# ConvFFN input part: five orders of the products of high and low parts, in turn by group of blocks

## Chip, cores and metric

The kernel runs on one core of one Trainium2 chip. The metric is the device time of one execution in microseconds. The kernel before takes 892.87 us, the median of 3 runs (892.58 to 893.33).

## The reference, cut to what matters

The program computes one layer of a hybrid encoder block on 512 frames of 1024 channels: two recurrent branches, a merge, cross-attention, and a gated ConvFFN, with a norm ahead of each and one at the end. The change lies in the input half of the ConvFFN:

```
def conv_ffn(h, w_in, conv_w, conv_b, w_out):
    u = h @ w_in                                  # (512 x 1024) @ (1024 x 5632)
    gate = causal_dwconv(u[..., :D_FF], conv_w, conv_b)
    return (jax.nn.gelu(gate) * u[..., D_FF:]) @ w_out
```

`D_FF` is 2816: a gate half and a value half of 22 blocks of 128 columns each. What is changed is in which order the matmuls of `h @ w_in` are issued.

## The kernel before

**Precision.** Each float32 operand is split into a high part (rounded to the matmul's input format) and a low part (the remainder). A product is made of three matmuls: high by high, high by low and low by high. `mm3` (line 165) issues the three in this order, with the weights first in each pair: lines 166 (weights high, moving operand high), 167 (weights high, moving operand low) and 168 (weights low, moving operand high). Each matmul comes with a load of its own weights.

**Seven products.** The input part multiplies in a Strassen-like scheme: the activations and weights are cut into two by two parts and seven products of sums of these are made instead of eight. Each product has a name by its weights: `A11`, `s1`, `s2`, `s4`, `s3`, `A12`, `A22`; the table `RHS` (line 1206) gives the activation operand of each (`hop`, tiles `hq` and `hr` in the profile, with high and low part of 4 tiles of 128x256 each).

**Groups.** The loop at line 1258 goes through the 22 blocks in 11 groups of `NQ = 2`. In a group, each product is made for block 0 and then for block 1. One product of one block is 4 steps in depth by 3 matmuls, 12 matmuls of 128x128 weights by 256 columns. So a group has 7 x 2 x 12 = 168 matmuls. The accumulators are in PSUM, for each block: `X` (`fx_ps`, 256 columns) and `YZ` (`fyz_ps`, 512 columns). `X` collects in turn A11, s2, s3 and A22, the second half of `YZ` s1 and s4, the first half A12. There are four of each, so that two groups are in flight. Between products the running state is copied out: ScalarE copies `X` after A11 (line 1266) and after s2 (line 1274) to `sn`, and the half of `YZ` after s1 (line 1269) to `p5`; VectorE adds `X` after s3 to `p5` (line 1279). Each next product onto the same tile must wait for that copy: s2 for 1266, s4 for 1269, s3 for 1274, A22 for 1279.

**Behind a group** VectorE and ScalarE make the convolution over time, the gelu (line 1293, ScalarE) and the product of gate and value (lines 1286 to 1297) while TensorE works on the next group.

**Weights.** `stream_quarters` (line 124) makes one load for each product of a group, that is, for both blocks: a DMA to `wfi_r` (four buffers), a cast on ScalarE to the high part `wfi_h` (line 132), a subtraction on VectorE for the low part `wfi_l` (line 133), three buffers each. A buffer is free for the load after next-but-one when TensorE has read it for the last time.

**Background sums.** The sums of weight parts for the coming products are made by accumulating DMAs on POOL. `sum_behind` (line 173) ties the next of these to a matmul, which paces them.

**Order.** A scheduler of the language orders the instructions of each engine by their dependencies, their place in the program and its own estimate of times; loads and their casts have high priority. The queues of the engines are worked off in that order.

Of the kernel before, what the change touches and what calls it, by code (L numbers as in the profile page):

```python
# [12 lines left out]
ALU = mybir.AluOpType  # L13
# [4 lines left out]
P = 128  # L18
T = 512
# [39 lines left out]
def hybrid_block_kernel(ctx: ExitStack, tc: tile.TileContext, xT_d, mT_d, pv_d, cst_d, win_d, wk_d, wv_d,  # L59
                        lup_d, gup_d, rga_d, rgx_d, wba_d, wbb_d, wmix_d, wq_d, wo_d, wfi_d, wfo_d, out_d):  # L60
    nc = tc.nc
    V, S, PE = nc.vector, nc.scalar, nc.tensor
# [26 lines left out]
    def par(name, i, n=1):  # L89
        o = PV[name][0]  # L90
        return pv[:, o + i:o + i + n]
# [32 lines left out]
    def stream_quarters(srcs, name):  # L124

        for g, src in enumerate(srcs):
            with tc.high_priority():
                raw = wp.tile([P, 2, T], F32, tag="wr", name=f"{name}_r{g}", bufs=4)
                wdma.append(nc.sync.dma_start(raw, src))
                hi = wp.tile([P, 2, T], F32R, tag="wh", name=f"{name}_h{g}")  # L130
                lo = wp.tile([P, 2, T], F32R, tag="wl", name=f"{name}_l{g}")
                S.copy(hi, raw)  # L132
                V.tensor_tensor(lo, raw, hi.bitcast(F32), ALU.subtract)  # L133
            for i in range(2):
                yield hi[:, i], lo[:, i]

    class Units:
# [10 lines left out]
        def next(self):  # L148
            if self.left == 0:
                self.fill()  # L150
            i = self.i
            self.i += 1
            self.left -= 1
            return self.hi[:, i * P:(i + 1) * P], self.lo[:, i * P:(i + 1) * P]
# [10 lines left out]
    def mm3(ps, lh, ll, rh, rl, start, stop, **kw):  # L165
        first = PE.matmul(ps, lh, rh, start=start, stop=False, **kw)  # L166
        PE.matmul(ps, lh, rl, start=False, stop=False, **kw)  # L167
        PE.matmul(ps, ll, rh, start=False, stop=stop, **kw)  # L168
        return first
# [3 lines left out]
    def sum_behind(ins, n=1):  # L173

        for put in islice(sums, n):
            tc.add_manual_dep(tc.keep_in_program_order(put()).ins, ins.ins.name, mybir.DependencyInfo(
                mybir.DependencyClass.Sync, mybir.DependencyReason.DATA), reason="pace of the sums")
# [89 lines left out]
    def rstd_bc(out, ssq, n, pool=None, scratch=None, load=True, split=None, **kw):  # L267

        ps = rw_ps("rs_ps", pool, **kw)
        if split is None:  # L270
            PE.matmul(ps[:, :n], ones, ssq, start=True, stop=True)
        else:
            sum_exact(ps[:, :n], onesr, ssq, *split)
        rsqrt(out, ps[:, :n], 1.0 / D, eps[:, 0:1], load)
        if scratch is not None:
            newton(out, ps[:, :n], scratch, 1.0 / D, 1e-6)
# [6 lines left out]
    with tc.tile_pool(name="p0", bufs=1, reuse_waits="tile") as p0:  # L283
# [103 lines left out]
        for hf in range(2):  # L387
            pss = [(mm_ps if hf else rw_ps)(f"v_ps{hf}_{i}") for i in range(2)]
            for k2 in range(4):
                wh, wl = next(st)  # L390
                for kk in range(2):
                    kb = 2 * k2 + kk
                    rh, rl = wh[:, kk * T:(kk + 1) * T], wl[:, kk * T:(kk + 1) * T]
                    for i in range(2):
                        sl = slice(i * P, (i + 1) * P)
# [72 lines left out]
    NQ = 2  # L468
# [269 lines left out]
    with tc.tile_pool(name="pz", bufs=1, reuse_waits="tile") as pz:  # L738
# [9 lines left out]
        for s in range(30, -1, -1):  # L748
            n = 31 - s
# [25 lines left out]
    for i0 in (0, 16):  # L775
# [3 lines left out]
        for i in range(16):  # L779
            for e in range(2):  # L780
                r, k = rows[0][e], rows[1][e]
                PE.matmul(psh[e][k, i * 32:(i + 1) * 32], BZ[r, i0 + i, 32:64], ZA[r, i0 + i, :],
                          start=True, stop=True)
        for e, copy in enumerate((S.copy, V.tensor_copy)):
            k = rows[1][e]
            copy(Hs[e][k], psh[e][k].rearrange("p (i t) -> p i t", t=32))
        for i in range(16):
            for e in range(2):
                r, k = rows[0][e], rows[1][e]
                PE.matmul(pso[e][r, i * 32:(i + 1) * 32], Hs[e][k, i, :], BZ[k, i0 + i, 32:64],  # L790
                          start=True, stop=True)
        for e, copy in enumerate((S.copy, V.tensor_copy)):
            r = rows[0][e]
# [355 lines left out]
    H = T // 2  # L1149
# [19 lines left out]
    for m in order:  # L1169
# [5 lines left out]
        i = m % 4  # L1175
# [32 lines left out]
    def source(m, n):  # L1208
        if n[0] == "A":
            return quarter(m, int(n[1]), int(n[2]), NQ)  # L1210
        return dS[m // NQ][:, :, SLOT[n], :].rearrange("n p f -> p n f")

    wq = stream_quarters([source(m, n) for m in range(0, FB, NQ) for n in RHS], "wfi")

    def product(n, out, start, nsum=0):
        wh, wl = next(wq)
        b = hop[RHS[n]]
        for i in range(4):
            sl = slice(i * P, (i + 1) * P)
            ins = mm3(out, wh[:, sl], wl[:, sl], b[:, 0, i, :], b[:, 1, i, :], start and i == 0, i == 3,  # L1220
                      skip_group_check=not start)
            if i < nsum:
                sum_behind(ins)

    graw = pc.tile([P, FB, T], F32, name="graw", bufs=1)
    gsets = [[pc.tile([P, n, 2, H], F32R, name=f"go0_{n}", bufs=1) for n in (8, 3)], [None, None], [None, None]]
# [7 lines left out]
    def split_g(i, src, k):  # L1236
        dst, n = part(i, k)
        S.copy(dst[:, :, 0, :], src(slice(k, k + n)))
        V.tensor_tensor(dst[:, :, 1, :], src(slice(k, k + n)), dst[:, :, 0, :].bitcast(F32), ALU.subtract)

    def g1(ks, c):
        return graw[:, ks, (c - 1) * H:c * H]
# [7 lines left out]
    def b1_g(k):  # L1250
        ks = slice(k, min(k + 4, HB))
        diff_g(g1(ks, 1), g1(ks, 1), g1(ks, 2))

    def b3_g(k):
        ks = slice(k, min(k + 4, HB))
        diff_g(g1(ks, 2), g2(ks, 2), g1(ks, 2))

    for m0 in range(0, FB, NQ):
        ms = range(m0, m0 + NQ)
        YZ = {m: pf.tile([P, T], F32, tag="yz", name=f"fyz_ps{m}", bufs=4) for m in ms}  # L1260
        X = {m: pf.tile([P, T], F32, tag="x", name=f"fx_ps{m}", bufs=4)[:, 0:H] for m in ms}
        sn = {m: pc.tile([P, T], F32, tag="sn", name=f"sn{m}", bufs=3) for m in ms}
        p5 = {m: pc.tile([P, H], F32, tag="p5", name=f"p5_{m}", bufs=3) for m in ms}
        for m in ms:
            product("A11", X[m], True, nsum=m - m0)
            S.copy(sn[m][:, 0:H], X[m])
        for m in ms:
            product("s1", YZ[m][:, H:T], True)
            S.copy(p5[m], YZ[m][:, H:T])
        if m0 == 0:  # L1270
            rstd_bc(rf, ssf, T, pf, split=(pc, "ac", "rf"), tag="yz", bufs=4)
        for m in ms:
            product("s2", X[m], False, nsum=m - m0)
            S.copy(sn[m][:, H:T], X[m])
        for m in ms:
            product("s4", YZ[m][:, H:T], False, nsum=m - m0)
        for m in ms:
            product("s3", X[m], False)
            V.tensor_tensor(p5[m], X[m], p5[m], ALU.add)
        for m in ms:  # L1280
            product("A12", YZ[m][:, 0:H], True, nsum=m - m0)
        for m in ms:
            product("A22", X[m], False, nsum=(m - m0) * (m0 // NQ % 2))
        for m in ms:
            s = pc.tile([P, T], F32, tag="s", name=f"fs{m}")
            V.tensor_tensor(s, YZ[m], sn[m], ALU.add)
            V.tensor_tensor(s, s, rf, ALU.mult)
            ac = pc.tile([P, T], F32, tag="ac", name=f"fa{m}")
            S.activation(ac, s, AF.Identity, scale=par("fcw", 44 + m), bias=par("fcb", m))
            for k in range(1, 3):  # L1290
                V.scalar_tensor_tensor(ac[:, k:], s[:, 0:T - k], par("fcw", 22 * (2 - k) + m), ac[:, k:],
                                       ALU.mult, ALU.add)
            gelu = S.activation(ac, ac, AF.Gelu_apprx_tanh)
            V.tensor_tensor(ac, ac, rf, ALU.mult)
            out = graw[:, m]
            V.scalar_tensor_tensor(out[:, 0:H], X[m], -1.0, ac[:, 0:H], ALU.mult, ALU.mult)
            V.scalar_tensor_tensor(out[:, H:T], p5[m], -1.0, ac[:, H:T], ALU.mult, ALU.mult)
            k = m % HB
            if k % 4 == 3 or k == HB - 1:
                k -= k % 4  # L1300
                if m < HB:
                    split_g(0, lambda ks: g1(ks, 1), k)
                    b1_g(k)
                else:
                    b3_g(k)
# [61 lines left out]
    X = [pf.tile([P, T], F32, tag="x", name=f"ox_ps{m}", bufs=4)[:, 0:H] for m in range(MQ)]  # L1367
    YZ = [pf.tile([P, T], F32, tag="yz", name=f"oyz_ps{m}", bufs=4) for m in range(MQ)]
    cols = (slice(0, H), slice(H, T))
    sn1, sn5 = ([pc.tile([P, T], F32, tag="sn", name=f"{n}_{i}", bufs=3) for i in range(2)] for n in ("o1", "o5"))  # L1370
    p1, p5 = ([t[:, c] for t in ts for c in cols] for ts in (sn1, sn5))
# [158 lines left out]
```

## Time and profile before

| what | value |
|---|---|
| median of 3 runs | 892.87 us |
| profiled execution, span | 892.8 us |
| TensorE busy | 877.4 us, 98% |
| VectorE busy | 685.2 us, 77% |
| ScalarE busy | 513.6 us, 58% |
| input part of the ConvFFN (first matmul of group 0 to first matmul of the output part) | 553.83 to 772.65 us |
| in it: matmuls of the products | 1848 |

All times are of one core. The profiled execution has no time of its own beside its span; the span agrees with the median to 0.1 us. The busy time of TensorE counts pipelined matmuls, so the distance between the starts of two matmuls is the cost of one and not its recorded duration. In lists in order of time the columns are the start in us, the duration in us, the engine, the line, the operation, output and inputs, shapes and count, and in brackets how long the engine was idle before it and what ended that.

### The profile page before, as it was taken

The numbers are of one execution on the slowest core, as the hardware profiler recorded it, in microseconds if no ns is written. First come the engines' busy times: TensorE is split into PE (matmuls) and PEld (weight loads), VectorE is DVE, ScalarE is ACT, GpSimd is POOL, SyncE is SP. The second block draws the span as 40 slices with busy tenths as digits, with TensorE's granted clock in tenths as the row PEclk, the third lists the DMA queues.
The fourth block names the chain that finished last, engine by engine and source line by source line (L and its number), as shares of the span: only waits on it lengthen the run. The fifth ranks groups of instructions, "written<-read, shape, count | busy, mean of one in ns | idle before, by whom it ended". The sixth has DMA issues, their size and how long they took to land.

```text
span 892.8 us, 15934 instructions
## 1 busy us (share of the span) xinstructions
PE 877.4 (98%) x6197; PEld 767.9 (86%) x6197; DVE 685.2 (77%) x1104; ACT 513.6 (58%) x783; POOL 132.5 (15%) x163
## 2 busy tenths in 40 slices
PE   8999999999999999999999999999999999999996
PEld 7878878888877677888888778999999999999996
DVE  6796598777967677675575578889888889999674
ACT  6575676634347676233554466766655656757563
POOL 0101222021102021001122111111111111211100
PEclk9999999999999999999999999999999999999999
DMA  7878899678997279758888958999999999998963
GB/s 268 307 253 215 206 228 233 187 203 233 262 227 156 72 203 249 220 166 229 218 234 183 197 137 185 260 275 271 265 255 294 263 297 275 244 276 220 261 202 94
DMA packets 97242, 201.37 MB, mean 226 GB/s; under 512 B 19536, under 2 KB 30928, under 8 KB 97104
## 3 DMA queue, kind: packets, MB, share of 16 engines
q1 hardware_dynamic: 62240, 118.57, 40.4%
q0 software_dynamic: 25504, 67.38, 36.9%
q10 hardware_dynamic: 9424, 14.42, 4.7%
q8 instruction: 48, 0.79, 0.4%
q14 instruction: 26, 0.21, 0.1%
HBM read 188.54 MB, written 78.12 MB: 299 GB/s over the span
## 4 chain that ended last, share of the span: by engine, by line
PE 91%; DVE 4%; DMA 2%; ACT 1%; issue 1%; DVEq 0%; ACTq 0%; SPq 0%
PE in_ps L167 7%; PE in_ps L166 7%; PE in_ps L168 7%; PE fx_ps L167 5%; PE fx_ps L166 5%; PE fx_ps L168 5%; PE fyz_ps L167 4%; PE fyz_ps L166 4%; PE fyz_ps L168 3%; PE ox_ps L166 2%; PE oyz_ps L166 2%; PE ox_ps L168 2%; PE oyz_ps L168 2%; PE oyz_ps L167 2%; PE ox_ps L167 2%; PE co_ps L167 2%
## 5 line engine op out<-in xcount | busy, mean ns | idle before, releaser
L132 ACT CAST wfi_h<-wfi_r 128x1024 fp32r<-128x1024 f32 x77 | 81.1, 1053 | 71.5 <-PE fx_ps L167 19.7
L168 PE MATMUL in_ps<-hT,win_l 128*128 128x512 f32 x304 | 121.3, 399 | 0.0
L167 PE MATMUL in_ps<-hT,win_h 128*128 128x512 f32 x304 | 121.0, 398 | 0.2 <-DVE hT L384 0.2
L166 PE MATMUL in_ps<-hT,win_h 128*128 128x512 f32 x304 | 120.6, 398 | 0.3 <-DVE pr L586 0.3
L133 DVE TENSOR_TENSOR wfi_l<-wfi_r,wfi_h 128x1024 fp32r<-128x1024 f32 x77 | 94.1, 1222 | 22.7 <-ACT wfi_h L132 22.4
L482 POOL DMA_DIRECT2D dS<-in_wfi x66 | 66.7, 1028 | 293.1 <-PE in_ps L166 102.3
L167 PEld LDWEIGHTS in_ps<-hT,win_h 128*128 128x128 f32 x304 | 57.1, 188 | 14.2 <-issue 0.7
L166 PEld LDWEIGHTS in_ps<-hT,win_h 128*128 128x128 f32 x304 | 57.1, 188 | 13.2 <-DVE pr L586 0.7
L168 PEld LDWEIGHTS in_ps<-hT,win_l 128*128 128x128 f32 x304 | 57.1, 188 | 13.1 <-issue 0.7
L518 POOL DMA_DIRECT2D dOs<-in_wfo x54 | 39.8, 784 | 181.5 <-PE fyz_ps L166 54.0
L118 DVE TENSOR_TENSOR win_l<-win_r,win_h 128x1024 fp32r<-128x1024 f32 x38 | 46.3, 1221 | 24.2 <-ACT win_h L117 20.7
L117 ACT CAST win_h<-win_r 128x1024 fp32r<-128x1024 f32 x38 | 39.9, 1050 | 41.1 <-PE in_ps L167 32.4
L1341 DVE TENSOR_TENSOR wfo_l<-wfo_r,wfo_h 128x1024 fp32r<-128x1024 f32 (+1 forms) x39 | 47.2, 1209 | 15.2 <-ACT wfo_h L1340 15.2
L1340 ACT CAST wfo_h<-wfo_r 128x1024 fp32r<-128x1024 f32 (+1 forms) x39 | 40.5, 1039 | 31.3 <-DMA wfo_r<-dOs 11.6
L168 PE MATMUL ox_ps<-go,wfo_l 128*128 128x256 f32 x176 | 49.1, 279 | 0.8 <-DVE wfo_l L1341 0.8
L166 PE MATMUL ox_ps<-go,wfo_h 128*128 128x256 f32 x176 | 49.2, 279 | 0.4 <-ACT wfo_h L1340 0.3
L166 PE MATMUL fx_ps<-hq,wfi_h 128*128 128x256 f32 x176 | 49.4, 280 | 0.0
L166 PE MATMUL fyz_ps<-hq,wfi_h 128*128 128x256 f32 x176 | 49.2, 280 | 0.0
L167 PE MATMUL fx_ps<-hq,wfi_h 128*128 128x256 f32 x176 | 49.2, 280 | 0.0
L167 PE MATMUL fyz_ps<-hq,wfi_h 128*128 128x256 f32 x176 | 49.2, 280 | 0.0
L167 PE MATMUL fx_ps<-hr,wfi_h 128*128 128x256 f32 x176 | 49.2, 280 | 0.0
L166 PE MATMUL fx_ps<-hr,wfi_h 128*128 128x256 f32 x176 | 49.2, 279 | 0.0
(432 smaller groups left out, 2704.9 us busy)
## 6 DMA issues: line engine op xcount, KB each, us to landing
dS<-in_wfi POOLq DMA_DIRECT2D x66, 512.0 KB, 7.8
wfi_r<-dS SPq DMA_DIRECT2D x44, 512.0 KB, 6.8
win_r<-in_win SPq DMA_DIRECT2D x38, 512.0 KB, 5.3
wfi_r<-in_wfi SPq DMA_DIRECT2D x33, 512.0 KB, 5.8
dS<-dS POOLq DMA_DIRECT2D x22, 512.0 KB, 5.7
dOs<-in_wfo POOLq DMA_DIRECT2D x12, 512.0 KB, 7.9
wk_r<-in_wk SPq DMA_DIRECT2D x8, 512.0 KB, 5.1
wv_r<-in_wv SPq DMA_DIRECT2D x8, 512.0 KB, 4.0
```

Of the source, the lines that this page charges most:

```text
L117: casts.append(S.copy(hi[:, o:o + n], raw[:, o:o + n]))
L118: V.tensor_tensor(lo[:, o:o + n], raw[:, o:o + n], hi[:, o:o + n].bitcast(F32), ALU.subtract)
L132: S.copy(hi, raw)
L133: V.tensor_tensor(lo, raw, hi.bitcast(F32), ALU.subtract)
L166: first = PE.matmul(ps, lh, rh, start=start, stop=False, **kw)
L167: PE.matmul(ps, lh, rl, start=False, stop=False, **kw)
L168: PE.matmul(ps, ll, rh, start=False, stop=stop, **kw)
L482: return lambda: nc.gpsimd.dma_start(s(out), src, **kw)
L518: yield lambda k=k, w=w, src=src: nc.gpsimd.dma_start(dO[n, m][:, k * P:(k + w) * P], src, **kw)
L1340: S.copy(hi[:, :n], raw[:, :n])
L1341: V.tensor_tensor(lo[:, :n], raw[:, :n], hi[:, :n].bitcast(F32), ALU.subtract)
```

## The change

The function `product` (one block, one product, through `mm3`) is replaced by `products`, which takes both blocks. The weights of both are fetched ahead of the first matmul (they come from one load). A table gives five orders of the 12 matmuls; a pair `(w, r)` names weights and moving operand, 0 for high and 1 for low, and `i` is the step in depth. The group's number modulo 5 picks the order, the *kind*:

- kind 0 (groups 0, 5, 10): for each `i` high-high, high-low, low-high, as before
- kind 1 (groups 1, 6): for each `i` high-high, low-high, high-low
- kind 2 (groups 2, 7): for each `i` high-high, high-low; then low-high for all `i`
- kind 3 (groups 3, 8): high-high for all `i`, high-low for all `i`, low-high for all `i`
- kind 4 (groups 4, 9): the order of kind 0, and the two blocks take turns matmul by matmul

The function is a generator: it yields a block when its last matmul is issued, and the caller makes the copy of that block there. The sums are tied to the first matmul of block 1 as before; in kind 4 this is the second matmul of the product, in the other kinds the 13th.

```
-    def product(n, out, start, nsum=0):
-        wh, wl = next(wq)
+    ORDER = {
+        0: [(i, p) for i in range(4) for p in ((0, 0), (0, 1), (1, 0))],
+        1: [(i, p) for i in range(4) for p in ((0, 0), (1, 0), (0, 1))],
+        2: [(i, (0, k)) for i in range(4) for k in range(2)] + [(i, (1, 0)) for i in range(4)],
+        3: [(i, p) for p in ((0, 0), (0, 1), (1, 0)) for i in range(4)],
+        4: [(i, p) for i in range(4) for p in ((0, 0), (0, 1), (1, 0))],
+    }
+
+    def products(n, outs, start, nsum=0):
+
+        ws = [next(wq) for _ in outs]
         b = hop[RHS[n]]
-        for i in range(4):
-            sl = slice(i * P, (i + 1) * P)
-            ins = mm3(out, wh[:, sl], wl[:, sl], b[:, 0, i, :], b[:, 1, i, :], start and i == 0, i == 3,
-                      skip_group_check=not start)
-            if i < nsum:
+        kind = ms[0] // NQ % 5
+        seq = ORDER[kind]
+        steps = [(m, k) for m in range(len(outs)) for k in range(len(seq))]
+        if kind == 4:
+            steps.sort(key=lambda s: s[1])
+        for m, k in steps:
+            i, (w, r) = seq[k]
+            ins = PE.matmul(outs[m], ws[m][w][:, i * P:(i + 1) * P], b[:, r, i, :], start=start and k == 0,
+                            stop=k == len(seq) - 1, **(dict(skip_group_check=True) if not start else {}))
+            if k == 0 and m == 1 and nsum:
                 sum_behind(ins)
+            if k == len(seq) - 1:
+                yield m
...
-        for m in ms:
-            product("A11", X[m], True, nsum=m - m0)
-            S.copy(sn[m][:, 0:H], X[m])
...
+        xs, hi, lo = [X[m] for m in ms], [YZ[m][:, H:T] for m in ms], [YZ[m][:, 0:H] for m in ms]
+        for k in products("A11", xs, True, 1):
+            S.copy(sn[m0 + k][:, 0:H], xs[k])
+        for k in products("s1", hi, True):
+            S.copy(p5[m0 + k], hi[k])
...
+        for k in products("s2", xs, False, 1):
+            S.copy(sn[m0 + k][:, H:T], xs[k])
+        for k in products("s4", hi, False, 1):
+            pass
+        for k in products("s3", xs, False):
+            V.tensor_tensor(p5[m0 + k], xs[k], p5[m0 + k], ALU.add)
+        for k in products("A12", lo, True, 1):
+            pass
+        for k in products("A22", xs, False, m0 // NQ % 2):
+            pass
```

More of the change, by code (lines that the diff above doesn't have):

```diff
@@ L1263, in hybrid_block_kernel @@
         p5 = {m: pc.tile([P, H], F32, tag="p5", name=f"p5_{m}", bufs=3) for m in ms}
-        for m in ms:
-            product("A11", X[m], True, nsum=m - m0)
-            S.copy(sn[m][:, 0:H], X[m])
-        for m in ms:
-            product("s1", YZ[m][:, H:T], True)
-            S.copy(p5[m], YZ[m][:, H:T])
+        xs, hi, lo = [X[m] for m in ms], [YZ[m][:, H:T] for m in ms], [YZ[m][:, 0:H] for m in ms]
[3 more added lines that the diff above has]
+            S.copy(p5[m0 + k], hi[k])
         if m0 == 0:
             rstd_bc(rf, ssf, T, pf, split=(pc, "ac", "rf"), tag="yz", bufs=4)
[L1272 to L1283, printed above, removed]
+        for k in products("s2", xs, False, 1):
[8 more added lines that the diff above has]
+            pass
         for m in ms:
```

## The prediction

> **What bounds the kernel now.** I read the profile's page first: the span, the busy times, the granted clock and the chain that ended last.
>
> ```profile
> span 892.8 us, 15934 instructions
> ...
> PE 877.4 (98%) x6197; PEld 767.9 (86%) x6197; DVE 685.2 (77%) x1104; ACT 513.6 (58%) x783; POOL 132.5 (15%) x163
> ...
> PEclk9999999999999999999999999999999999999999
> ...
> PE 91%; DVE 4%; DMA 2%; ACT 1%; issue 1%; DVEq 0%; ACTq 0%; SPq 0%
> ```
>
> TensorE is busy 98% of the span, is 91% of the chain, and has its full clock. So a change to its matmuls can count in two ways only: another distance from one matmul to the next, or other waits between them. The page's busy shares cannot tell those apart, since one pipelined matmul overlaps the next. I therefore read the busy time of the changed stage alone (PE, PEld, DVE, ACT, POOL, then clock and DMA), and then the order of time, where the distance between starts is what a matmul costs.
>
> ```profile
> 553.83:772.65 218.82, 218.82 (x1852) 218.33 (x1850) 193.32 (x263) 138.19 (x203) 35.86 (x49) 1.00 0.94 268
> ```
>
> ```profile
> 553.83 0.28 PE L166 MATMUL fx_ps<-hq,wfi_h 128*128 128x256 f32 x1
> 553.95 0.28 PE L167 MATMUL fx_ps<-hq,wfi_h 128*128 128x256 f32 x1
> 554.07 0.28 PE L168 MATMUL fx_ps<-hq,wfi_l 128*128 128x256 f32 x1
> 554.18 0.28 PE L166 MATMUL fx_ps<-hq,wfi_h 128*128 128x256 f32 x1
> ...
> 642.43 0.28 PE L166 MATMUL fyz_ps<-hq,wfi_h 128*128 128x256 f32 x1
> ...
> 662.22 0.28 PE L166 MATMUL fyz_ps<-hq,wfi_h 128*128 128x256 f32 x1
> ```
>
> The columns are start, duration, engine, line. A matmul is recorded with 0.28 us but the next starts 0.12 us later. The last two rows are the same matmul (first of product s4) of groups 4 and 5, one group of 7 x 24 = 168 matmuls apart: 19.79 / 168 = 0.1178 us a step. The stage has 11 x 168 = 1848 of them: 217.7 us. Two matmuls of the norm with 512 columns (0.23 us each, as the 512-column rows below) make it 218.2 of 218.82. The stage thus loses about 0.65 us to waits. That is all that an order can win back unless the step itself changes.
>
> **The step: does the order change it?** The new orders differ from the old in three things: how often a weight tile is followed by itself, how often a moving operand is, and whether neighbours write one accumulator or two. For each the trace of before has a neighbour.
>
> Weights, and low parts at the end of the product (kind 2's order): the first stage has one block of 128x256 matmuls in just that order, 16 with high weights (line 184), then 8 with low ones (line 186).
>
> ```profile
> 12.80 2.05 PE L184 MATMUL k_ps<-m,wk_h 128*128 128x256 f32 x16
> 14.68 1.10 PE L186 MATMUL k_ps<-m,wk_l 128*128 128x256 f32 x8
> 15.62 0.28 PE L166 MATMUL k_ps<-m,wk_h 128*128 128x256 f32 x1
> ```
>
> Sixteen steps in 1.88 us and eight in 0.94 us: 0.1175 us both, where weights repeat in pairs and where they never do. The four rows at 553.83 say the same: the second matmul keeps its weights, the third and fourth change them, at 0.12, 0.12 and 0.11 us. Repeated weights are loaded again anyhow (6197 loads for 6197 matmuls on the page). So kind 2, which keeps the repeats, and kinds 1, 3 and 4, which lose them all, neither win nor lose by the weights: 0.
>
> The moving operand held while the weights change (4 of 12 steps in kind 1, 12 of 24 in kind 4, none before): lines 608 and 609 do that with 512 columns.
>
> ```profile
> 102.06 0.39 PE L608 MATMUL psw<-pwa,lhi 128*128 128x512 f32 x1
> 102.28 0.40 PE L609 MATMUL psw<-pwa,llo 128*128 128x512 f32 x1
> 102.52 0.39 PE L608 MATMUL psa<-pwa,lhi 128*128 128x512 f32 x1
> ```
>
> With the operand held it is 0.22 us to the next, with a new one 0.24. The rows are rounded to 0.01 at either end; the nearest row says no difference, and 0.02 us in 0.23 is the most it could be. By that most, 256 columns would win 0.01 us; two groups have 336 / 3 = 112 such steps in kind 1 and 168 in kind 4, 0 to -2.8 us together. I take 0.
>
> Two accumulators in turn (kind 4): a 512-column matmul, two 256-column ones into another bank, and the first bank again.
>
> ```profile
> 504.66 0.40 PE L167 MATMUL co_ps<-o,wo_h 128*128 128x512 f32 x1
> 504.90 0.40 PE L1111 MATMUL sc_ps<-K,q 128*128 128x256 f32 x2
> 505.13 0.40 PE L168 MATMUL co_ps<-o,wo_l 128*128 128x512 f32 x1
> ```
>
> ```profile
> 503.45:505.60 2.15, 2.15 (x13) 1.83 (x13) 1.65 (x4) 0.00 (x0) 1.15 (x1) 1.00 1.07 132
> ```
>
> It is 0.24 us, then 0.23 for the two: the steps of unmixed rows, with clock 1.00 in that stretch. 0 again. The Trainium skill has a rule against such alternation ("TensorE: Matmul & The Clock Gate", section "A second HAM failure mode: psum-queue depth-cycling"): a kernel that went round its banks let the array idle briefly and often enough that the clock gate swung between half and full. By that rule kind 4 would be slower; the stretch above, though only a few switches long, does not show it.
>
> **The waits: where kind 4 gives up cover.** Kinds 0 to 3 finish block 0 after 12 matmuls and block 1 after 24, as before. Kind 4 (groups 4 and 9) finishes both at the end and, what counts more, begins both at once. A product that accumulates onto a tile must wait until ScalarE has copied the tile's earlier state (lines 1266, 1269, 1274). For block 1 the 12 matmuls of block 0 (1.41 us) lie ahead of that wait today; in kind 4 one does (0.12 us). TensorE takes its queue in order, so all matmuls of the stage stand behind it. In group 9 even today's cover is used up:
>
> ```profile
> 739.05 0.39 ACT L1269 COPY p<-fyz_ps 128x256 f32<-128x256 f32 x1
> ...
> 741.91 0.63 ACT L1293 ACTIVATE fa<-fa 128x512 f32<-128x512 f32 x1 [1.52 <-DVE fa L1291]
> 742.45 0.36 ACT L1269 COPY p<-fyz_ps 128x256 f32<-128x256 f32 x1
> 742.70 0.38 ACT L1274 COPY sn<-fx_ps 128x256 f32<-128x256 f32 x1
> ```
>
> ```profile
> 741.36 0.28 PE L166 MATMUL fyz_ps<-hq,wfi_h 128*128 128x256 f32 x1
> ...
> 742.66 0.28 PE L168 MATMUL fyz_ps<-hq,wfi_l 128*128 128x256 f32 x1
> 742.86 0.39 PE L166 MATMUL fyz_ps<-hq,wfi_h 128*128 128x256 f32 x1
> 743.09 0.28 PE L167 MATMUL fyz_ps<-hq,wfi_h 128*128 128x256 f32 x1
> ...
> 744.38 0.28 PE L166 MATMUL fx_ps<-hr,wfi_h 128*128 128x256 f32 x1
> ```
>
> Block 1's copy of s1 stands behind the gelu of the group before (line 1293), which waits for VectorE; it starts at 742.45, and s4's first matmul of block 1 follows 0.41 us later at 742.86. Today that costs 0.43 - 2 x 0.118 = 0.19 us. In kind 4 block 0's s1 result comes just one matmul ahead of block 1's, so I put both copies behind the gelu: block 0's at 742.45, block 1's at 742.70. Then s4 begins at 742.86 instead of 741.36, block 1's first matmul at 742.70 + 0.41 = 743.11, 22 more steps end the product, and s3 begins at 743.11 + 23 x 0.1178 = 745.82 instead of 744.38: **+1.44 us**. Were block 0's copy still ahead, block 1's first matmul at 742.86 would give +1.19.
>
> Group 4 has the same queue, but in time:
>
> ```profile
> 640.64 0.63 ACT L1293 ACTIVATE fa<-fa 128x512 f32<-128x512 f32 x1
> 641.17 0.35 ACT L1269 COPY p<-fyz_ps 128x256 f32<-128x256 f32 x1
> 641.42 0.38 ACT L1274 COPY sn<-fx_ps 128x256 f32<-128x256 f32 x1
> ```
>
> The second copy would end at 641.80, and s4 starts at 642.43: 0.6 us of cover is left, cost 0. Were its gelu as late as group 9's against its own s4 (742.45 - 741.36 = 1.09 us after, not 1.26 before), it would cost 1.44 too.
>
> The edits with one answer: both weight halves are fetched ahead of the first matmul, but they come from one load, so no DMA or cast moves in its queue; kinds 2 and 3 let the high tile go 3 steps (0.35 us) earlier and ask for the low one 6 steps (0.7 us) later, kind 1 holds the high tile one step longer and asks for the low one a step earlier, kind 4 lets the high one go a step earlier and asks for the low one two later. With 0.65 us of waits in the whole stage none of this is on the path; bounds -0.65 (all waits gone) to 14 tiles x 2 groups x 0.12 = +3.3 us (kind 1 wholly exposed); taken as 0. The background sums on POOL start 11 steps earlier in kind 4, off the path.
>
> **What is late next.** Behind the stage TensorE waits once for VectorE's line 1296:
>
> ```profile
> 784.11 0.42 DVE L1296 SCALAR_TENSOR_TENSOR graw<-fx_ps,fa 128x256 f32<-128x256 f32 x1
> ```
>
> ```profile
> 784.19 0.28 PE L168 MATMUL ox_ps<-go,wfo_l 128*128 128x256 f32 x1
> 784.58 0.39 PE L166 MATMUL ox_ps<-go,wfo_h 128*128 128x256 f32 x1
> 784.81 0.28 PE L167 MATMUL ox_ps<-go,wfo_h 128*128 128x256 f32 x1
> ```
>
> It is 0.62 us for two steps, a wait of 0.38. VectorE works off a backlog there, so a TensorE that comes 1.4 us later should not meet it: -0.38 (at worst 0). **Sum:** 1.44 - 0.38 = +1.06 us on the profiled execution's 892.8 us, which is within 0.1 us of the median 892.87. **Forecast 893.9 us.** Two runs of this kernel can be told apart from about 0.2%, 1.8 us; the forecast is no change.
>
> **The rivals.** (1) *Nothing at all*: the scheduler, which orders each engine's queue by its own reckoning, puts the copies ahead of the gelu, or the backlog of group 9 does not form. The scheduler does put matmuls of other tiles between two of one (line 1111 above), so the turns themselves may not come out as written. For it: in group 4 the same queue is in time. Sum 0 to -0.65 in the stage: 892.2 to 892.8. Chance 0.27. (2) *Slower*: kind 4's lost cover is hit in both its groups, and in s2 or s3 besides s4; price 1.44 each, two or three times, 2.9 to 4.3 us less 0.38: 895.3 to 896.7. It decides as soon as group 4's copies come 0.6 us later against its s4. Against it: the rows of group 4. Chance 0.18. (3) *Faster*: the step is not bound by columns alone and a held moving operand cheapens it. The early half-clock rows give a bound:
>
> ```profile
> 9.18 0.41 PE L166 MATMUL k_ps<-m,wk_h 128*128 128x256 f32 x1
> 9.39 0.41 PE L167 MATMUL k_ps<-m,wk_h 128*128 128x256 f32 x1
> ```
>
> ```profile
> 9.18:11.52 2.34, 2.34 (x12) 2.34 (x12) 2.34 (x7) 2.34 (x6) 0.00 (x0) 0.50 1.04 412
> ```
>
> At clock 0.50 a step is 0.21 us; half of that is 0.105, so some 0.012 us of the 0.1178 is not explained by the clock. Won on the 112 + 168 steps with a held operand it makes -3.4 us: 889.4. Lines 608 and 609 speak against it. Chance 0.08. (4) *The clock swings in kind 4*: 336 matmuls at 0.21 instead of 0.118 are +31 us, 924; the stretch at clock 1.00 speaks against it. Chance 0.02. (This is what the skill's rule above would give.)
>
> **How the numbers follow.** The forecast has 0.45: own range 893.2 to 894.4 (with and without the 0.38, copies 1.19 or 1.44). No change within 0.2%: 0.45 + 0.27 = 0.72. Slower: 0.18 + 0.02 = 0.20. Faster: 0.08. For 8 in 10 the range takes in cases 0 and 1 and the lower half of 2: 892.2 to 895.6.
>
> **What would show it.** Right: steps of 0.118 us in all five kinds; both copies of s1 in group 9 behind the gelu and s4 starting some 1.4 us late; no such wait in group 4; the 0.38 us wait at the start of the output part gone. Wrong: any kind whose 168 matmuls take other than 19.8 us without a wait in them; a granted clock under 1 in groups 4 and 9; waits for weights in kind 1.

## The result, and the profile after

The changed kernel takes 899.75 us, the median of 3 runs (897.52 to 900.89), against 892.87: a ratio of 1.0066, with a 95% interval of 1.0044 to 1.0089. It is slower, outside the predicted range of 892.2 to 895.6. A second set, of 10 runs, gave 898.61 against 894.45, a ratio of 1.0053 [1.0034, 1.0072].

The page after, with the lines that answer to those shown of before, and the row of the output part's first matmuls:

```profile
span 895.7 us, 15931 instructions
...
PE 877.6 (98%) x6197; PEld 768.2 (86%) x6197; DVE 685.3 (77%) x1104; ACT 513.8 (57%) x783; POOL 132.8 (15%) x163
...
PEclk9999999999999999999999999999999999999998
...
PE 86%; DVE 6%; DMA 5%; ACT 2%; issue 1%; DVEq 0%; ACTq 0%; SPq 0%
...
L166 PE MATMUL ox_ps<-go,wfo_h 128*128 128x256 f32 x176 | 49.2, 280 | 2.9 <-DVE graw L1307 2.9
```

TensorE has the same busy time and the same number of matmuls, but VectorE and DMA have gained a share of the chain. The last row names the place: 2.9 us idle ahead of an `ox_ps` matmul, for VectorE's line 1307. (The change moves the lines: 1296 of before is 1307 after, 1291 is 1302, 1294 is 1305, 1239 is 1253, 1341 is 1352, and copy 1269 is 1282.) This execution's own time was 897.52, that is 1.8 us above its span. The same holds for the runs whose time and span are both known, so before's profiled execution with its span of 892.8 took some 894.6, not the 892.87 of the median.

The stage itself (column by column as in the prediction: PE, PEld, DVE, ACT, POOL, clock, DMA, GB/s), and then the first part of the output product:

```profile
552.22:772.19 219.97, 219.33 (x1852) 218.47 (x1851) 192.61 (x263) 138.26 (x203) 35.98 (x49) 1.00 0.94 267
772.19:779.96 7.77, 7.77 (x68) 7.72 (x66) 7.77 (x10) 5.90 (x8) 3.27 (x5) 1.00 0.98 274
```

The stage takes 219.97 us, 1.15 more than before, at full clock. Every group without a wait takes 19.79 us, in all five kinds. In group 9 (kind 4) both copies of s1 stand behind the gelu, as forecast, but TensorE loses only 0.65 us in that group. Of ScalarE, then of TensorE:

```profile
739.88 0.64 ACT L1304 ACTIVATE fa<-fa 128x512 f32<-128x512 f32 x1 [1.26 <-DVE fa L1302]
740.43 0.63 ACT L1282 COPY p<-fyz_ps 128x256 f32<-128x256 f32 x2
```

```profile
740.20 0.40 PE L1234 MATMUL fx_ps<-hq,wfi_l 128*128 128x256 f32 x2
740.83 0.89 PE L1234 MATMUL fyz_ps<-hq,wfi_h 128*128 128x256 f32 x4 [0.23 <-ACT p L1282]
```

The other 0.68 us lies in group 2 (kind 2), where block 1's s3 waits for the copy of line 1286. That it is kind 2's is not shown: in an execution with kind 0 in all groups the same place lost 0.84 us (the forced order below). Behind the stage:

```profile
779.84 0.28 PE L168 MATMUL ox_ps<-go,wfo_l 128*128 128x256 f32 x1
783.05 0.38 PE L166 MATMUL ox_ps<-go,wfo_h 128*128 128x256 f32 x1 [2.93 <-DVE graw L1307]
783.27 0.28 PE L167 MATMUL ox_ps<-go,wfo_h 128*128 128x256 f32 x1
```

From 779.84 to 783.05 are 3.21 us for one step of 0.12: a wait of 3.09 us where before had 0.38. Why, VectorE's rows tell: first before, then after.

```profile
778.17 0.69 DVE L1294 TENSOR_TENSOR fa<-fa,rf 128x512 f32<-128x512 f32 x1
778.77 0.74 DVE L1291 SCALAR_TENSOR_TENSOR fa<-fs,pv,fa 128x510 f32<-128x510 f32 x1
779.43 0.42 DVE L1296 SCALAR_TENSOR_TENSOR graw<-fx_ps,fa 128x256 f32<-128x256 f32 x1
...
784.11 0.42 DVE L1296 SCALAR_TENSOR_TENSOR graw<-fx_ps,fa 128x256 f32<-128x256 f32 x1
```

```profile
777.78 1.40 DVE L1302 SCALAR_TENSOR_TENSOR fa<-fs,pv,fa 128x510 f32<-128x510 f32 x2
779.10 1.22 DVE L1253 TENSOR_TENSOR go<-graw,go 128x1024 fp32r<-128x1024 f32 x1
780.24 1.22 DVE L1352 TENSOR_TENSOR wfo_l<-wfo_r,wfo_h 128x1024 fp32r<-128x1024 f32 x1
781.37 1.28 DVE L1305 TENSOR_TENSOR fa<-fa,rf 128x512 f32<-128x512 f32 x2
782.58 0.42 DVE L1307 SCALAR_TENSOR_TENSOR graw<-fx_ps,fa 128x256 f32<-128x256 f32 x1
782.91 0.41 DVE L1308 SCALAR_TENSOR_TENSOR graw<-p,fa 128x256 f32<-128x256 f32 x1
783.25 0.42 DVE L1307 SCALAR_TENSOR_TENSOR graw<-fx_ps,fa 128x256 f32<-128x256 f32 x1
```

The output part has four blocks of `X` (`ox_ps`) in the four banks that the input part's `fx_ps` used. Its third and fourth block take the banks of the last group. Each is free once VectorE has read `fx_ps` in line 1307 (1296 before). Before, the read for the third block came at 779.43, ahead of its use, and only the one for the fourth was 0.38 us late. After, VectorE's queue is *another order*: both blocks go through each step in pairs, and a split for the output part (line 1253) and one of weights (line 1352) stand ahead of the first read, which starts at 782.58. VectorE has not one idle gap in these rows, so an instruction moved ahead is time for whoever stands behind it. The diff does not touch a line of VectorE's there. So the scheduler chose another order for instructions that the change leaves as they were. That its estimate of times tipped with the new order of matmuls is an inference; the estimate itself is in no trace.

### The profile page after: what moved, and what is told of

Its sections match the earlier page's. It is cut to its first block, busy times and chain, and to the rows that moved or that the text cites. A ratio compares the mean times of both kernels' runs of the same rounds, so it can differ in the third digit from the quotient of the medians.

```text
span 895.7 us, 15931 instructions
## 1 busy us (share of the span) xinstructions
PE 877.6 (98%) x6197; PEld 768.2 (86%) x6197; DVE 685.3 (77%) x1104; ACT 513.8 (57%) x783; POOL 132.8 (15%) x163
## 4 chain that ended last, share of the span: by engine, by line
PE 86%; DVE 6%; DMA 5%; ACT 2%; issue 1%; DVEq 0%; ACTq 0%; SPq 0%
PE fx_ps L1234 13%; PE fyz_ps L1234 10%; PE in_ps L167 7%; PE in_ps L166 7%; PE in_ps L168 7%; DMA wfo_r<-dOs 2%; PE co_ps L167 2%; PE co_ps L166 2%; PE q_ps L167 2%; PE co_ps L168 2%; PE mix_ps L168 2%; PE q_ps L168 2%; PE q_ps L166 2%; PE mix_ps L167 2%; PE mix_ps L166 2%; PE ox_ps L168 1%
## 5 line engine op out<-in xcount | busy, mean ns | idle before, releaser
L1234 PE MATMUL fx_ps<-hr,wfi_h 128*128 128x256 f32 x352 | 57.1, 280 | 0.4 <-ACT sn L1286 0.4
L1234 PE MATMUL fyz_ps<-hq,wfi_h 128*128 128x256 f32 x352 | 57.2, 280 | 0.2 <-ACT p L1282 0.2
L1234 PE MATMUL fx_ps<-hq,wfi_h 128*128 128x256 f32 x352 | 57.4, 280 | 0.0
L1234 PEld LDWEIGHTS fyz_ps<-hq,wfi_h 128*128 128x128 f32 x352 | 49.6, 188 | 0.6 <-ACT p L1282 0.4
L1234 PEld LDWEIGHTS fx_ps<-hr,wfi_h 128*128 128x128 f32 x352 | 49.5, 188 | 0.6 <-ACT sn L1286 0.6
L1234 PEld LDWEIGHTS fx_ps<-hq,wfi_h 128*128 128x128 f32 x352 | 49.7, 188 | 0.2
```

The source lines that it names most:

```text
L1234: ins = PE.matmul(outs[m], ws[m][w][:, i * P:(i + 1) * P], b[:, r, i, :], start=start and k == 0, stop=k == len(seq) - 1, **(dict(skip_gro ...
```

## Experiments

Unless said otherwise the edit is one line of the changed kernel, the choice of the kind; waits are counted as distance less one step.

**The changed kernel again**, unaltered.

> The changed kernel once more, unaltered, to see what of its loss repeats. Both theories: steps of 0.1178 us in all kinds. Theory Q (order of the other engines' queues): the wait of some 3 us of the output part's third block for VectorE's read of the last group's accumulator comes again, and the time is 4 to 8 us over the kernel before. Theory C (kind 4's lost cover, the prediction's): the waits in groups 4 and 9 make most of the loss, and the wait of the output part is an accident of one execution and goes.

898.61 us (10 runs) against 894.45 (27): 1.0053 [1.0034, 1.0072]. The profiled execution was its fastest, 891.77, and still waits 3.09 us at the same place (775.44 to 778.65), and 1.85 us in group 9. Where its speed is from is told below ("What was not expected").

**Kind 4 alone, and all kinds but 4.** The first has kind 0 in all groups but 4 and 9, the second kinds 0 to 3, with kind 0 in groups 4 and 9.

```
-        kind = ms[0] // NQ % 5
+        kind = ms[0] // NQ % 5 // 4 * 4      # kind 4 alone
+        kind = ms[0] // NQ % 5 % 4           # all but 4
```

> Kind 4 in groups 4 and 9, kind 0 in all others. The scheduler's order of VectorE's last group is then the one of the changed kernel: block 0's accumulator is read only behind block 1's last steps. Theory Q: about the whole loss of the changed kernel stays, 4 to 7 us, with a wait of 2.5 to 3.5 us at the third block of the output part. Theory C: 1 to 2 us, in group 9. A third theory, that kinds 1 to 3 cost by themselves: no more than 1 us here.

> Kinds 0 to 3 as in the change, groups 4 and 9 of kind 0. VectorE's queue is that of the kernel before but for four pairs of neighbours, with the same tail. Theories Q and C: within 1 us of the kernel before, no wait over 0.6 us at the third block of the output part. Third theory (kinds 1 to 3 cost): 3 us or more.

Kind 4 alone has the whole loss: 899.54 us, 1.0051 [1.0034, 1.0068], a wait of 3.09 at the output part and 0.21 in group 9. Without it there is none: 894.32, 0.9995 [0.9984, 1.0006]. VectorE's and TensorE's rows without kind 4:

```profile
777.10 0.74 DVE L1302 SCALAR_TENSOR_TENSOR fa<-fs,pv,fa 128x510 f32<-128x510 f32 x1
777.76 0.42 DVE L1307 SCALAR_TENSOR_TENSOR graw<-fx_ps,fa 128x256 f32<-128x256 f32 x1
...
782.44 0.42 DVE L1307 SCALAR_TENSOR_TENSOR graw<-fx_ps,fa 128x256 f32<-128x256 f32 x1
```

```profile
782.41 0.28 PE L168 MATMUL ox_ps<-go,wfo_l 128*128 128x256 f32 x1
782.91 0.39 PE L166 MATMUL ox_ps<-go,wfo_h 128*128 128x256 f32 x1 [0.22 <-DVE graw L1307]
```

That is before's order in VectorE's queue and before's wait of 0.38. So kinds 1, 2 and 3 cost and win nothing that can be measured.

**Which group?** Kind 4 in group 9 alone, and in group 4 alone.

```
+        kind = 4 * (ms[0] // NQ == 9)
+        kind = 4 * (ms[0] // NQ == 4)
```

> Kind 4 in group 9 alone. VectorE's queue of the last group is the changed kernel's. Theory Q: the 3 us wait, and 3 to 5 us over the kernel before. If kind 4 costs by its own matmuls or cover, half of the loss of two groups: about 2.5 us.

> Kind 4 in group 4 alone. VectorE's queue of the last group is that of the kernel before. Theory Q: within 0.5 us of the kernel before, no wait over 0.5 us at the third block of the output part. If kind 4 costs by its own matmuls or cover, half of the loss of two groups: about 2.5 us.

Group 9 alone: 899.56 us, 1.0072 [1.0045, 1.01], a wait of 3.25. That is 6.0 us over the kernel before, more than the 3 to 5 expected; the half clock of the last runs below is part of it. Group 4 alone: 893.44, 0.9999 [0.9984, 1.0014], a wait of 0.63 at the fourth block as in before. The same edit costs everything in one group and nothing in the other.

**VectorE's queue set by hand, with all five kinds kept.** The last steps of block 21 and the splits for the output part are held behind the reads.

```
+            behind = tc.issue_after(read.ins) if m == FB - 1 else nullcontext()
             for k in range(1, 3):
-                V.scalar_tensor_tensor(...)
+                with behind if k == 2 else nullcontext():
+                    V.scalar_tensor_tensor(...)
...
     def prepare(i, src):
+        with tc.issue_after(reads[FB - 1].ins):
```

> The changed kernel with VectorE's queue of the last group pinned: block 0's read of its accumulator stands ahead of block 1's second step of the convolution, and the splits for the output part behind block 1's read. Theory Q: the 3 us wait goes, the time falls by 2.5 to 3.5 us against the changed kernel. Theory C: it falls by less than 0.5 us.

896.06 us, 1.0012 [0.9999, 1.0025]: most of the loss is gone, and so is the wait at the third block. Another one came later, for VectorE's line 1394; the splits that were held back stand ahead of it in VectorE's queue:

```profile
803.51 0.28 PE L168 MATMUL oyz_ps<-go,wfo_l 128*128 128x256 f32 x1
805.20 0.36 PE L166 MATMUL oyz_ps<-go,wfo_h 128*128 128x256 f32 x1 [1.41 <-DVE t L1394]
```

So the mended order still pays 1.57 us.

**The banks exchanged, with all five kinds kept.** The output part's `X` takes the banks of `fyz_ps`, which VectorE frees early in a group's tail (in the profile after it reads `fyz_ps` at 769.51 and `fx_ps` only from 782.58 on), and `YZ` those of `fx_ps`. The order is left to the scheduler, and kind 4 stays where it is.

```
-    X = [pf.tile([P, T], F32, tag="x", name=f"ox_ps{m}", bufs=4)[:, 0:H] for m in range(MQ)]
-    YZ = [pf.tile([P, T], F32, tag="yz", name=f"oyz_ps{m}", bufs=4) for m in range(MQ)]
+    X = [pf.tile([P, T], F32, tag="yz", name=f"ox_ps{m}", bufs=4)[:, 0:H] for m in range(MQ)]
+    YZ = [pf.tile([P, T], F32, tag="x", name=f"oyz_ps{m}", bufs=4) for m in range(MQ)]
...
```

Three more lines, left out here, exchange the tags of the last norm's tiles in the same way.

> The changed kernel with the accumulators of the output part taken from the other tags: its first product writes into the banks that held YZ in the last group, which VectorE reads some 10 us earlier, and its second into those of X. Orders and arithmetic are the changed kernel's. Theory Q (the loss is the wait for X's banks behind VectorE's late read): the 3 us wait goes without another in its place, 3 to 4 us less than the changed kernel, 0 to 1.5 us over the kernel before (group 9's waits). Theory C (lost cover in groups 4 and 9): still 3 us or more over it.

895.07 us, 1.0002 [0.9986, 1.0019]. In the profile VectorE's read is as late as after the change, and TensorE doesn't wait for it any more:

```profile
786.05 1.28 DVE L1305 TENSOR_TENSOR fa<-fa,rf 128x512 f32<-128x512 f32 x2
787.25 1.21 DVE L1352 TENSOR_TENSOR wfo_l<-wfo_r,wfo_h 128x1024 fp32r<-128x1024 f32 x1
788.39 0.41 DVE L1307 SCALAR_TENSOR_TENSOR graw<-fx_ps,fa 128x256 f32<-128x256 f32 x1
```

Group 9 loses 1.06 us there, more than in the profile after, and yet no loss can be measured. (The profiled execution was the slowest of the 12, 899.11 us, with a mean granted clock of 0.945; its changed stage begins at 556.48 us instead of 552.22.)

**The exchanged banks with kind 0 everywhere**, as a candidate for a faster kernel, in two sets.

> The same exchange of banks with kind 0 in all groups, which is the kernel before but for the banks. Theory Q: its 0.38 us wait goes, 0.2 to 0.6 us faster than the kernel before. Theory C says nothing of it.

> The kernel with exchanged banks and kind 0 in all groups once more, for its interval: 0.2 to 0.7 us faster than the kernel before if the 0.38 us wait was all that it lost there; within 0.2 us if VectorE's backlog takes it back later.

893.2 us, 0.9992 [0.9978, 1.0005], and 893.08, 0.9999 [0.9982, 1.0017]. The wait of 0.38 is gone in the profile, but that is less than these sets can tell. No version here measurably beats before.

**The order of VectorE forced on the old order of matmuls.** Kind 0 everywhere; in the last group both reads are queued behind block 21's product (line 1305), as the scheduler had done by itself after the change.

```
-            V.tensor_tensor(ac, ac, rf, ALU.mult)
+            mul = V.tensor_tensor(ac, ac, rf, ALU.mult)
+            if m == FB - 2:
+                held = ac
+                continue
+            with ExitStack() as late:
+                if m == FB - 1:
+                    late.enter_context(tc.issue_after(mul.ins))
...
```

> Kind 0 in all groups, and in the last group both blocks' reads of their accumulators are queued on VectorE behind block 1's last multiplication, as the scheduler did it in the changed kernel; one split for the output part comes ahead of them too. TensorE's order is the kernel before's. Theory Q: block 0's read comes 2.9 us later than before, a wait of about 2.3 us at the third block of the output part, none at the fourth; the time 1.5 to 2.5 us over the kernel before. If only the order of the products mattered: within 0.5 us of it.

897.56 us, 1.0045 [1.003, 1.006]: the loss without a single matmul in another place. The stage's matmuls stand as before. Of VectorE, then of TensorE:

```profile
779.40 1.23 DVE L1253 TENSOR_TENSOR go<-graw,go 128x1024 fp32r<-128x1024 f32 x1
780.54 1.23 DVE L1359 TENSOR_TENSOR wfo_l<-wfo_r,wfo_h 128x1024 fp32r<-128x1024 f32 x1
781.67 0.69 DVE L1305 TENSOR_TENSOR fa<-fa,rf 128x512 f32<-128x512 f32 x1
782.27 0.43 DVE L1314 SCALAR_TENSOR_TENSOR graw<-fx_ps,fa 128x256 f32<-128x256 f32 x1
```

```profile
780.20 0.28 PE L168 MATMUL ox_ps<-go,wfo_l 128*128 128x256 f32 x1
782.75 0.39 PE L166 MATMUL ox_ps<-go,wfo_h 128*128 128x256 f32 x1 [2.27 <-DVE graw L1314]
```

The wait is 2.43 us, that is 2.05 more than before, and the kernel loses 4.0, more than the 1.5 to 2.5 expected. The last runs show a part of the rest.

**One kind everywhere**: kind 1, and kind 4.

```
+        kind = 1
+        kind = 4
```

> Kind 1 in all groups, no kind 4 and no lost cover. In VectorE's queue of the last group three more pieces of 1.13 us stand ahead of block 0's read of its accumulator than before, and block 1's read is later as well. Theory Q: a wait of 2.5 to 3 us at the third block of the output part and up to 1 us at its fourth; the time 2 to 4 us over the kernel before. Theory C, and any theory by which kind 1 itself is neutral: within 0.5 us of it.

> Kind 4 in all groups. Theory Q: block 0's read is on time in VectorE's queue of the last group, block 1's some 3 us late, so that the wait comes at the fourth block of the output part, 2.5 to 3.5 us; besides, the lost cover shows where a copy had less than 1.3 us in hand before (groups 0, 2, 7 and 9), 1 to 4 us in all: 3 to 7 us over the kernel before. Theory C: the cover's share alone, 5 us or more from waits inside the groups. If matmuls that take turns between two banks were slower by themselves: steps over 0.1178 us and 10 us or more.

Kind 1 everywhere takes 897.04 us, 1.0026 [1.0014, 1.0038], although kind 1 in groups 1 and 6 cost nothing: the scheduler gives VectorE a late order here too, and TensorE's rows show a wait of 2.62 us.

```profile
781.20 0.28 PE L168 MATMUL ox_ps<-go,wfo_l 128*128 128x256 f32 x1
783.94 0.39 PE L166 MATMUL ox_ps<-go,wfo_h 128*128 128x256 f32 x1 [2.46 <-DVE graw L1307]
```

It has no two accumulators in turn, so it is the queue and not kind 4 as such. Kind 4 everywhere takes 900.71 us, 1.0077 [1.006, 1.0095], and by another way than expected: no long wait at the output part, but about half a microsecond in nearly every group, where s4's block 1 waits for copy 1282. Group 8 lost 4.0 us in the profiled execution (the slowest, 905.03 us): s4 waited 1.25 and, one matmul later, 1.15 us, and half clock followed. Lost cover is real, then; with kind 4 in two groups it is the small part.

**Four more executions**, profiled, on one chip: the changed kernel twice, the forced order (kind 0) once, and before once.

> The changed kernel, one more look. The wait of the third output block is again 3 us or more. Theory Q alone: nothing follows it, and the waits over those of the kernel before add to 3 to 4 us. Theory H (half clock): where the wait passes some 3.2 us, the matmuls behind it start at 0.213 instead of 0.1178 us for some 3 to 4 us, which costs 1.4 us more.

> The same as the look before it: theory H expects the half-clock stretch in some of these looks and a time 1 to 2 us longer in those, theory Q in none.

> The kernel with VectorE's late reads and kind 0, one more look: a wait of 2.3 to 2.6 us at the third output block. Theory H: no half-clock stretch behind so short a wait, and its further loss comes from other waits.

> The kernel before, one more look, for what its waits are in another execution: 0.3 to 0.7 us at the fourth output block, and no half-clock stretch after the first 12 us.

The times were 898.09, 898.09, 898.36 and 888.51 us; another run of before on this chip took 894.64. The changed kernel waits 4.14 and 3.57 us in them, and behind that wait its clock drops. The stretch behind the wait of the second execution, and then that of the forced order, where the wait was 2.59 and no drop was expected:

```profile
782.55:787.84 5.29, 5.29 (x25) 5.29 (x26) 4.55 (x7) 1.78 (x2) 0.84 (x1) 0.50 0.87 292
```

```profile
783.75:787.10 3.35, 3.35 (x18) 3.35 (x17) 3.19 (x4) 1.62 (x2) 0.00 (x0) 0.51 1.02 330
```

In the first row, at a granted clock of 0.50, 24 steps take 5.29 us instead of 24 x 0.1178 = 2.83, some 2.5 us more. The other execution of the changed kernel loses 1.6 us so, the forced order 1.5, and kind 4 in group 9 alone 1.6 (18 steps in 3.76 us):

```profile
783.46:787.28 3.82, 3.82 (x19) 3.82 (x20) 3.27 (x6) 1.78 (x2) 0.00 (x0) 0.55 0.98 318
```

The kernel after in the first profile, its first repetition and kind 4 alone show no such stretch behind 3.09 us. The wait thus has a surcharge that comes in some executions. The granted clocks of all runs show it without a profile. Their mean is 0.9948 in the 10 runs of the changed kernel against 0.9963 in the 27 of before beside them: estimated as that difference times some 896 us, 1.3 us a run. In the same way it is 2.2 us with kind 4 in group 9 alone (0.9935 against 0.9960), and 0.9 us for the forced order (0.9950 against 0.9960). Of the forced order's 4.0 us the wait has 2.05 and the clock some 0.9; the last microsecond stays open.

## Why the prediction was wrong, point by point

**The step that failed is "What is late next".** It took VectorE's queue in the last group as fixed ("a TensorE that comes 1.4 us later should not meet it") and booked -0.38 us. The wait grew to 3.09, 3.09, 4.14 and 3.57 us in the four profiled executions, since the scheduler built another queue for VectorE. The prediction had in hand that the scheduler orders each engine by its own reckoning, and used it for TensorE's and ScalarE's queues only. That the queue is the cause is shown from both sides: forced without any change to the matmuls it costs 0.45%, and with the banks exchanged its late read costs nothing that can be measured. Why the scheduler's estimate tips for kind 4 in group 9 (and for kind 1 everywhere) and not for kind 4 in group 4 stays open; only that it does was seen.

**The lost cover of kind 4** was rightly placed, and at s4 forecast too large. Forecast were 1.44 us over the 0.19 of before; s4 lost 0.65, 0.82, 0.76 and 1.08 us in the four profiled executions of the changed kernel. In two of them s2 lost another 1.03 and 0.76, waiting for copy 1280, which the forecast priced at nothing, so that group 9 lost 0.65, 1.85, 0.76 and 1.84 in all. In the variants with kind 4 there it lost 0.21 to 1.06. The gelu's place to TensorE varies: it started 2.4 to 3.6 us behind the start of s1's last matmul in these four, so one profile's margin is one draw. Group 4 lost nothing in three of them and 0.37 in one; its price was 0, as forecast. Rival 2 had the waits at s2 besides s4, but rested on that cover alone; its time (895.3 to 896.7) is the nearest to what was measured, 2 to 4 us short of it, and for the wrong reason: exchanging the banks leaves the cover lost and ends at 1.0002.

**The step** was right: 19.79 us a group in all five kinds, so nothing by repeated weights, a held moving operand or banks in turn. Rival 3 fell with that, and rival 4 too: a clock of 1.00 over the whole stage after. The Trainium skill's rule on rounds through banks ("TensorE: Matmul & The Clock Gate", section "A second HAM failure mode: psum-queue depth-cycling"), told there for bf16 with 512 columns, is not borne out here, with 336 matmuls in turn at 0.1178 us. The clock did halve, but behind a wait.

**The baseline.** The prediction set its sum on the span of 892.8 us as if it were a time. Time is span plus 1.8, so the profiled execution was itself 1.8 us above the median. This shifts the forecast and not its sign. Its own range of 893.2 to 894.4 does not follow from its terms either: 892.8 + 1.19 - 0.38 and 892.8 + 1.44 are 893.6 and 894.2.

**The balance.** In microseconds, for the profiled executions of the two kernels as they are; "0.1133 steps" is what the matmuls from the stage on won by a shorter step (see "Two lengths of a step" below):

| execution | span | group 9 | wait at output part | half clock behind it | 0.1133 steps |
|---|---|---|---|---|---|
| before | 892.8 | 0.19 | 0.38 | 0 | -1.0 |
| before, again | 886.7 | 0 | 0.37 | 0 | -6.0 |
| after | 895.7 | 0.65 | 3.09 | 0 | 0 |
| after, again | 890.0 | 1.85 | 3.09 | 0 | -6.0 |
| after, third | 896.3 | 0.76 | 4.14 | 1.6 | -3.1 |
| after, fourth | 896.3 | 1.84 | 3.57 | 2.5 | -2.9 |

With the last column put back the spans are 893.8 and 892.7 before, and 895.7, 896.0, 899.4 and 899.2 after: means of 893.2 and 897.6, 4.4 us apart. Of these the wait at the output part has 3.47 - 0.38 = 3.1, the half clock behind it 1.0 on average, group 9 another 1.2. That is 5.3; the other -0.9 is not pinned down: the stage began between 552.2 and 553.8 us in these six executions, and another group waited up to 1.3 us in one of before and 0.7 in one of after. The two measured sets differ by 6.9 and 4.2 us.

## What to carry to other kernels

Under a scheduler that orders every engine by its own estimate, a change to one engine's order can change all queues: compare the queues of the engines that the diff does not touch, before and after, and look first where one of them has no slack. At a border between two stages ask which instruction frees the accumulators of the next stage, and give that stage banks that come free early; that cost nothing measurable here and took away a wait of 3 us. And read a cover of a few tenths of a microsecond as a draw from several executions, not as a margin.

## What was not expected of the hardware

**Two lengths of a step at one granted clock.** The same 95 us of the stage, from 592 to 687 us, in before's profile, in the second profile of before, and in that of the exchanged banks with all five kinds:

```profile
592.00:687.00 95.00, 95.00 (x809) 95.00 (x808) 86.64 (x117) 59.23 (x87) 16.20 (x23) 1.00 0.93 267
```

```profile
592.00:687.00 95.00, 95.00 (x841) 95.00 (x840) 87.75 (x120) 59.72 (x87) 16.95 (x25) 1.00 0.97 282
```

```profile
592.00:687.00 95.00, 95.00 (x808) 94.95 (x808) 86.68 (x117) 59.40 (x87) 16.20 (x23) 0.95 0.92 267
```

There are 841 matmuls instead of 809 at a clock of 1.00: 0.1133 us a step instead of 0.1178, 19.04 us a group instead of 19.79. Only TensorE's step differs: VectorE's splits of 1024 columns (line 133) take 1222 ns on average in both. The third row has a clock of 0.95 and the longer step all the same, so the granted clock does not tell the two apart. Both kernels show the shorter step, the changed one in all kinds, in stretches of some 17 to 150 us; it made the changed kernel's fastest run (891.77 us) and the fastest of before (888.51). What sets it is open. It is worth up to 6 us of an execution, and a single profile of either kernel could have told the wrong story.

**The clock behind a wait.** TensorE went to half clock behind waits of 3.25, 3.57 and 4.14 us and behind one of 2.59; it did not behind three of 3.09, nor behind 2.43 and 2.62. The length alone does not decide. In each trace with several changes of the granted clock these lie whole multiples of 3.413 us apart: with kind 4 in group 9 alone at 8.88, 12.30, 783.71 and 787.12 us, that is 1, 226 and 1 of them. Cut into stretches of that length, counted from such a change, the forced order with its waits of 2.59 and 2.43 us has these two, and the change with 3.57 and 3.09 the next two; the clock dropped at the end of the first one of each pair:

```profile
780.39:783.80 3.41, 1.10 (x9) 1.10 (x10) 3.41 (x8) 1.66 (x3) 0.55 (x2) 1.00 1.08 281
780.93:784.34 3.41, 1.59 (x13) 1.59 (x14) 3.41 (x7) 1.66 (x3) 0.00 (x0) 1.00 1.10 282
```

```profile
777.63:781.05 3.42, 1.50 (x13) 1.30 (x12) 3.42 (x5) 3.27 (x5) 1.67 (x3) 1.00 0.93 280
778.48:781.89 3.41, 1.64 (x14) 1.43 (x13) 3.41 (x5) 3.24 (x5) 1.52 (x3) 1.00 1.01 277
```

TensorE's busy time in the stretch (the second number) separates the cases of these waits: with a drop 0.08, 0.32, 1.10 and 1.50 us, and 1.44 for the two waits with kind 4 everywhere; without one, taking the idler of the stretches that a wait touches, 1.59, 1.64, 1.66, 1.70 and 2.15. So where a wait lies against these stretches counts as much as its length. It is a reading of ten cases and not a limit: at the start and the end of the kernels drops followed stretches with up to 1.8 us of busy time. The Trainium skill ("TensorE: Matmul & The Clock Gate", section "What's actually happening") has the clock halved after an idle window of some 3.4 us that runs freely. That the changes lie on one grid and that waits of one length differ agrees with a window that runs freely; that stretches with 1.1 to 1.5 us of work in them were enough is less idleness than the page's figure.
